# The last token group's projections traced whole before the early expert blocks, and the expert inputs loaded behind that group's weights

## The chip, the cores and the metric

The kernel runs on one core of one Trainium2 chip. The metric is the device time of one launch in microseconds, the median of three runs. A profiled execution is a further run of the same program under the hardware profiler.

## The reference, cut to what matters

One inference step of one layer of a hybrid decoder for 1024 prompt tokens and 32 sample tokens (8 sequences of 4), T = 1056 tokens of width 1024:

```
z = rmsnorm(x) @ w_in
h = x + [ rwkv7_mix(z_rwkv) | pool_mix(z_pool) ] @ w_out
xn = rmsnorm(h)
q = (xn @ peer_wq).reshape(tokens, 8 heads, 2, 128)
s1, s2 = q[:, :, 0] . keys[0],  q[:, :, 1] . keys[1]        # 128 keys each
v1, i1 = top_k(s1, 16);  v2, i2 = top_k(s2, 16)
sc, ci = top_k(v1 + v2 over all 256 pairs, 16)
expert = i1[ci // 16] * 128 + i2[ci % 16];  gate = softmax(sc)
act = gelu(u_tab[expert] . xn) * gate
h = h + sum over (8 heads x 16 experts) act * v_tab[expert]
h = h + (p @ ple_w) * sigmoid(rmsnorm(h) @ ple_gate_w)
y = rmsnorm(h)
```

So each token uses 128 of 16384 experts, and each expert is a row of u_tab and a row of v_tab, 1024 numbers each. Outputs are y for both sets of tokens and the new shift, wkv and pool states.

## The kernel before, in words

**Tiling and stages.** The 1056 tokens are the columns of most matmuls, in four groups (`GROUPS`, columns 0 to 288, 288 to 544, 544 to 800, 800 to 1056). The width of 1024 lies in 8 blocks of 128 partitions (`KB` = 8). A product that must be exact to fp32 is made as three matmuls of split operands: an operand is split into a part `hi` (a copy by ScalarE, ACT) and a rest `lo` or `elo` (a subtraction on VectorE, DVE, or on GpSimd, POOL), and the products hi·hi, hi·lo and lo·hi are summed (`mm3`, L649 to L660; `emm`, L1103 to L1110).

1. Stage a makes z for all tokens, stage b runs the wkv recurrence in chunks and leaves the mixed rows y in DRAM (`y_d`).
2. `phase_c(gi)` (from L680) takes one group of tokens: it loads y (L687), splits it, multiplies by the 8 column blocks of w_out (`wblock`, then `mm3`), adds the products into h (L700), normalises (L714), splits again and multiplies by the 16 column blocks of peer_wq; every 4 of these give two heads, whose scores against the keys (L743) go to DRAM (`sc_d`, L747). `wblock` loads pre-split weights from DRAM on the SyncE queue, SP (`whi`, L646, and `wlo`, L647). For the last six blocks of the last group (`b >= C3E`, `C3E` = 18) it loads unsplit weights (`eraw`, L1084) and splits them on the chip with `esplit`, the subtraction on POOL (`PTT`, L125).
3. `top` (from L749) takes one tile of up to 128 tokens: it reads the scores back (`scq`, L762), finds the 16 best of each head with DVE instructions (L765 to L770), the 16 best pairs, the gates, and, for the 672 "dense" tokens (columns below `GB`), the dense gate matrix. That matrix, 128 experts of a block by 128 blocks, is made for four tokens at a time, here called a quad: DVE builds one-hot factors (`ab`, L898) and two products (L899 and L900; the second, in two quads of three, on POOL, L125), PE multiplies them (8 matmuls, L903), ACT copies the result out (`gst`, L905), and every 32 tokens go to DRAM (`g_d`, L907). The tiles of dense tokens begin at columns 0, 128, 256, 288, 416, 544; the one at 544 has 128 tokens, 32 quads.
4. Expert blocks: there are 128 u-blocks of 128 experts and 16 groups of 8 v-blocks. A u-block (`ublock`, L1112 to L1116) splits 128 rows of u_tab (`eraw` from `uT`, 128x1024), makes 48 calls of the matmul line in `emm` against the normalised inputs `XH`, `XL` of the 672 dense tokens (two halves of 336 columns, shown as x2: 48 matmuls in all), and writes gelu of the sum to a tile `OT0` to `OT7` or `wt` (L1116). `ugate` (L1161) multiplies it by the dense gates, read back from DRAM (`gq`, L1164; L1167), and splits it (`wh` L1169 on ACT, `wl` L1171 on DVE). `vblock` (L1174) makes the 48 matmuls of a v-block from `wh` and `wl` of 8 u-blocks; the first v-block needs the gates of u-blocks 0 to 7.
5. The other 384 tokens fetch their expert rows one by one with indirect DMAs on POOL (L1219) and use DVE for the products (L1227 and L1236); this runs beside the expert blocks. A tail with the last gate and norms ends the kernel.

**What sets the order.** The kernel is written as Python generators. `merge` steps several of them in turn, each in proportion to its stated length, while the instructions are traced. The step loop (L1123 to L1150) does so for the stages: in step s the chunks of stage b, the tiles of `top` of group s − 2, and `phase_c(s - 1)`. A list scheduler then takes the traced instructions in traced order as priorities and places them per engine by a model of when their inputs are ready, so the order on an engine can differ from the traced one. Buffers come from pools with a fixed number of slots: `eraw` has 3, `ehi` and `elo` 2 each, the PSUM tiles `pd` of `emm` 2. The statement `with tc.issue_after(ins)` keeps the instructions traced inside it behind `ins` on the same queue.

**The place of the change.** In the last step (`step == NG`, 4) the tiles of group 2 are stepped to their end first; their pool is closed; then `phase_c(3)` (stated length 24) and `upre()`, which traces u-blocks 0 to 7, are merged (L1134 to L1141). Ahead of that, at the end of step 3, the 16 loads of `XH` and `XL` (128x672 each, 0.34 MB) are issued (L1147 to L1149). The loads come from `xh_d` and `xl_d`, where `phase_c(0)` to `phase_c(2)` have written the normalised, split inputs. After the step loop, `dense` traces u-blocks, gates and v-blocks.

Of the kernel before, what the change touches and what calls it, by code (L numbers as in the profile page):

```python
# [10 lines left out]
F32 = mybir.dt.float32  # L11
# [9 lines left out]
KB = D // 128  # L21
# [41 lines left out]
def body(ctx, tc, io):  # L63
    nc = tc.nc
# [12 lines left out]
    xh_d = dram.tile([128, KB, ND], F32, name="xh_d")  # L77
    xl_d = dram.tile([128, KB, ND], F32, name="xl_d")
    sc_d = dram.tile([sum(-(-(b - a) // 128) for a, b in GROUPS), 128, 16, 128], F32, name="sc_d")
    h2_d = dram.tile([128, KB, GT], F32, name="h2_d")  # L80
    wc_d = dram.tile([KB + 16, 128, 2, KB, 128], F32, name="wc_d")
# [380 lines left out]
    def bchunk(c, sp=None):  # L462
# [171 lines left out]
        PTT(yo, yo, fo, op=ALU.add)  # L634
        nc.sync.dma_start(y_d[:, :, pos:pos + tt], yo[:, :, :tt])

    def wblock(gi, b):
        if b >= C3E and gi == NG - 1:
            hi, lo = esplit(io["wq"][b - KB], PTT)
            return [(t[0], t[1]) for t in zip(*[(x[:, :HK], x[:, HK:]) for x in (hi, lo)])]  # L640
        out = []
        for i in range(1 if b < KB else 2):
            ks = slice(i * HK, (i + 1) * HK)
            hi = ws.tile([128, HK, 128], F32R, name="whi", bufs=3)
            lo = ws.tile([128, HK, 128], F32R, name="wlo", bufs=3)
            nc.sync.dma_start(hi.bitcast(F32), wc_d[b, :, 0, ks, :])  # L646
            nc.sync.dma_start(lo.bitcast(F32), wc_d[b, :, 1, ks, :])  # L647
            out.append((hi, lo))
        return out  # L649

    def mm3(ps, w, x, n):
# [257 lines left out]
    NG = len(GROUPS)  # L909
# [164 lines left out]
    NPRE = 8  # L1074
# [7 lines left out]
    def esplit(src, sub=TT):  # L1082
        raw = dr.tile([128, KB, 128], F32, name="eraw", bufs=3)
        nc.sync.dma_start(raw, src)  # L1084
        hi = dr.tile([128, KB, 128], F32R, name="ehi", bufs=2)
        ACT(hi, raw, AF.Copy)  # L1086
        lo = dr.tile([128, KB, 128], F32R, name="elo", bufs=2)
        sub(lo, raw, hi.bitcast(F32), op=ALU.subtract)  # L1088
        return hi, lo
# [28 lines left out]
    def upre():  # L1118
        for b in range(NPRE):
            ublock(b, PTT)  # L1120
            yield

    CL = [0, 24, 24, 24, 24]  # L1123
    for step in range(1, NG + 1):
        streams = []
        if step < NG:
            c_ = BC[step + 2:step + 4]
            streams.append((b_len(*c_), b_stream(*c_)))
        if 0 <= step - 2 < NG:
            streams.append((t_len(step - 2), t_stream(step - 2)))  # L1130
        if 0 <= step - 1 < NG:
            streams.append((CL[step], phase_c(step - 1)))
        if step == NG:
            for _ in streams[0][1]:  # L1134
                pass
            gstack.close()
            late = ctx.enter_context(tc.tile_pool(name="late", bufs=1, side="right", reuse_waits="tile"))
            gqp = ctx.enter_context(tc.tile_pool(name="gqp", bufs=2, side="right", reuse_waits="tile"))
            streams = [streams[1], (NPRE, upre())]
        merge(streams)  # L1140
        if step == NG - 1:  # L1141
            nc.sync.dma_start(io["wkv_p"], S[-1])
            pbx.close()
            dr = ctx.enter_context(tc.tile_pool(name="dr", bufs=1, side="right", reuse_waits="tile"))
            dps = ctx.enter_context(tc.tile_pool(name="dps", bufs=2, side="right", space=bass.MemoryType.PSUM, reuse_waits="tile"))
            XH, XL = xsplit()
            for k in range(KB):  # L1147
                nc.sync.dma_start(XH[:, k, :].bitcast(F32), xh_d[:, k, :])
                nc.sync.dma_start(XL[:, k, :].bitcast(F32), xl_d[:, k, :])  # L1149
            xs = [(XH[:, k, :], XL[:, k, :]) for k in range(KB)]  # L1150
    def gtop(col):
        for _ in top(tk, GB + col, min(128, GT - col)):
# [170 lines left out]
    XH, XL = xsplit()  # L1323
# [95 lines left out]
```

## Time and profile before

| | us |
|---|---|
| time before, median of 3 runs | 3339.67 |
| lowest and highest of them | 3336.93, 3353.06 |
| the profiled execution, device time | 3365.37 |
| its span in the trace | 3363.7 |
| mean granted TensorE clock in it | 0.968 |

| stage, us of the span | what runs |
|---|---|
| up to 1179 | stages a and b, `phase_c(0)` to `phase_c(2)`, the tiles of groups 0 and 1 up to the middle of tile 416 |
| 1179 to 1374 | rest of tile 416, `phase_c(3)`, tile 544, u-blocks 0 to 6 |
| 1374 to 1413 | last projections of `phase_c(3)`, u-blocks 7 and 8 |
| 1413 to 3205 | expert blocks, with the tiles of the 384 other tokens and then the gathers beside them |
| 3205 to 3364 | last expert blocks, tail |

How to read it: times are in microseconds from the start of the span unless marked ns. PE is TensorE, PEld its weight loads. A row of the timeline gives start, duration, engine, line, operation, output and input; what stands in brackets at its end is the time the engine was idle before it and what ended that wait. A row of the windows gives a stretch, its length, the busy time and number of instructions of each engine (PE, PEld, DVE, ACT, POOL, in this order), the granted TensorE clock, the busy share of the 16 DMA engines and GB/s.

### The profile page before, as it was taken

Reading aid. Unit: us, or ns where it says so; the run is one execution under the profiler, and the core shown is the slowest. Engines: PE = TensorE matmul, PEld = TensorE weight load, DVE = VectorE, ACT = ScalarE, POOL = GpSimd, SP = SyncE. Lnnn points to the kernel's source line nnn. Section 1 sums busy time; section 2 is a strip of 40 time slices with the busy share of each in tenths; the row PEclk is TensorE's granted clock in tenths of the full one; section 3 lists DMA queues with packets and bytes.
Section 4 is the critical chain, followed back from the end, with each engine's and each line's share of the span. In section 5 each row is a group of like instructions: output and inputs, shape, how many; then the busy total and the mean of one; then the engine's idle time right before and its main releaser. Section 6 shows DMA issues by size and latency. Waiting matters only on the chain.

```text
span 3363.7 us, 66962 instructions
## 1 busy us (share of the span) xinstructions
PE 3145.6 (94%) x26777; PEld 3006.4 (89%) x26777; DVE 2585.2 (77%) x5124; ACT 1128.8 (34%) x1734; POOL 1736.5 (52%) x1439
## 2 busy tenths in 40 slices
PE   8997799896998988899999999999999999999997
PEld 7886688786787877899999999999999999999997
DVE  6766322229799879899898888888889888888966
ACT  6452322223555555431221222222222222222243
POOL 5433232215446455327666665566566566666634
PEclk9998899997999989999999999999999999999998
DMA  4668544665776796739999999999999999999933
GB/s 160 203 219 195 145 130 127 204 191 149 235 217 201 232 317 204 244 109 371 343 330 332 343 349 328 333 334 339 337 336 349 326 330 342 338 329 337 323 107 127
DMA packets 448856, 879.89 MB, mean 262 GB/s; under 512 B 110240, under 2 KB 233376, under 8 KB 444064
## 3 DMA queue, kind: packets, MB, share of 16 engines
q1 hardware_dynamic: 337952, 472.91, 43.8%
q0 software_dynamic: 110592, 402.70, 32.9%
q8 instruction: 210, 3.44, 0.4%
q14 instruction: 102, 0.84, 0.1%
HBM read 754.89 MB, written 120.60 MB: 260 GB/s over the span
## 4 chain that ended last, share of the span: by engine, by line
PE 54%; DVE 7%; DMA 2%; issue 1%; ACT 0%; POOL 0%; SPq 0%; ACTq 0%; DVEq 0%; POOLq 0%
PE pd L1110 53%; DVE ab L898 1%; DMA row<-u,idx 1%; DVE elo L1088 1%; DVE oh L850 0%; DMA scq<-sc_d 0%; DMA eraw<-wq 0%; DVE OT L1316 0%; DVE ab L899 0%; DVE I L766 0%; DVE s L768 0%; DVE tg L1302 0%; DVE I L770 0%; DMA g_d<-gst 0%; DMA gq<-g_d 0%
## 5 line engine op out<-in xcount | busy, mean ns | idle before, releaser
L1219 POOL DMA_INDIRECT row<-v,idx x384 | 530.6, 1382 | 330.8 <-DVE po L1236 150.9
L1219 POOL DMA_INDIRECT row<-u,idx x384 | 542.5, 1413 | 274.9 <-DVE row L1227 107.4
L1086 ACT ACTIVATE ehi<-eraw 128x1024 fp32r<-128x1024 f32 x278 | 294.5, 1060 | 1095.9 <-PE pd L1110 976.8
L1110 PE MATMUL pd<-XH,elo 128*128 128x336 f32 x2176 | 515.3, 318 | 5.9 <-POOL elo L125 4.7
L1110 PE MATMUL pd<-XL,ehi 128*128 128x336 f32 x2176 | 515.1, 317 | 0.0
L1110 PE MATMUL pd<-XH,ehi 128*128 128x336 f32 x2176 | 512.4, 316 | 0.4 <-ACT ehi L1086 0.4
L1110 PE MATMUL pd<-wh,ehi 128*128 128x336 f32 (+1 forms) x2112 | 504.1, 317 | 6.6 <-DVE tg L1300 6.2
L1110 PE MATMUL pd<-wl,ehi 128*128 128x336 f32 (+1 forms) x2112 | 504.0, 317 | 0.0
L1110 PE MATMUL pd<-wh,elo 128*128 128x336 f32 (+1 forms) x2112 | 503.9, 317 | 0.2 <-DVE elo L1088 0.2
L1236 DVE SCALAR_TENSOR_TENSOR po<-row,act,po 128x1024 f32<-128x1024 f32 x381 | 488.5, 1282 | 6.8
L1227 DVE SCALAR_TENSOR_TENSOR row<-row,xt 128x1024 f32<-128x1024 f32 x384 | 455.7, 1219 | 9.7 <-DMA row<-u,idx 9.5
L1110 PEld LDWEIGHTS pd<-XH,elo 128*128 128x128 f32 x2176 | 373.5, 188 | 7.1 <-POOL elo L125 5.5
L1088 DVE TENSOR_TENSOR elo<-eraw,ehi 128x1024 fp32r<-128x1024 f32 x256 | 318.3, 1243 | 77.2 <-ACT ehi L1086 69.0
L1110 PEld LDWEIGHTS pd<-XH,ehi 128*128 128x128 f32 x2176 | 372.9, 189 | 0.9 <-ACT ehi L1086 0.6
L1110 PEld LDWEIGHTS pd<-XL,ehi 128*128 128x128 f32 x2176 | 371.3, 188 | 0.2
L1110 PEld LDWEIGHTS pd<-wh,ehi 128*128 128x128 f32 x2112 | 362.6, 188 | 7.6 <-issue 7.4
L1110 PEld LDWEIGHTS pd<-wh,elo 128*128 128x128 f32 x2112 | 362.7, 188 | 0.6 <-DVE elo L1088 0.5
L1110 PEld LDWEIGHTS pd<-wl,ehi 128*128 128x128 f32 x2112 | 362.8, 188 | 0.0
L125 POOL TENSOR_TENSOR ab<-ab,e 128x512 f16<-128x512 f16 x110 | 130.1, 1185 | 180.6 <-DVE ab L899 139.0
L657 PE MATMUL ps<-hi,whi 128*128 128x256 f32 (+1 forms) x592 | 185.7, 315 | 29.3 <-DMA whi<-wc_d 15.8
L1179 DVE TENSOR_TENSOR OT<-pd,OT 128x672 f32<-128x672 f32 x120 | 102.9, 857 | 140.7 <-PE pd L1110 139.8
L905 ACT ACTIVATE gst<-ps 128x512 f32<-128x512 f32 x168 | 174.9, 1089 | 85.5 <-PE ps L903 78.4
(428 smaller groups left out, 5526.9 us busy)
## 6 DMA issues: line engine op xcount, KB each, us to landing
eraw<-uT SPq DMA_DIRECT2D x128, 512.0 KB
eraw<-vP SPq DMA_DIRECT2D x128, 512.0 KB
g_d<-gst SPq DMA_DIRECT2D x21, 2048.0 KB
gq<-g_d SPq DMA_DIRECT2D x32, 1344.0 KB
whi<-wc_d SPq DMA_DIRECT2D x148, 256.0 KB
wlo<-wc_d SPq DMA_DIRECT2D x148, 256.0 KB
fdc<-fd SPq DMA_DIRECT2D x16, 896.0 KB
wc_d<-shi SPq DMA_DIRECT2D x40, 256.0 KB
```

Of the source, the lines that this page charges most:

```text
L125: nc.gpsimd.tensor_tensor(out, a, b, op=op)
L657: mm(ps[:, :n], whi[:, kk, :], xhi[:, k, :n], start=k == 0, stop=False)
L898: TT(ab[:, 0:4], iota16[:, None, :, :].to_broadcast([128, 4, EB, 2]), pairs(0, 4), op=ALU.is_equal)
L905: ACT(st[:, :, t2:t2 + 4].rearrange("p e t -> p t e"), v3(ps, 128), AF.Copy, scale=1.0 / GS)
L1086: ACT(hi, raw, AF.Copy)
L1088: sub(lo, raw, hi.bitcast(F32), op=ALU.subtract)
L1110: mm(ps[:, a, :n], w_[:, k, :], x_[:, s:s + n], start=first, stop=last)
L1179: TT(halves(OT[db]), ps[:, :, :NH], halves(OT[db]), op=ALU.add)
L1219: nc.gpsimd.indirect_dma_start(out=r[:m], out_offset=None, in_=io[tab], in_offset=bass.IndirectOffsetOnAxis(ap=idx[:m, hh, k:k + 1], axis=0))
L1227: STT(r[:m], r[:m], 1.0, xt[:m], op0=ALU.mult, op1=ALU.mult, accum_out=pre[:m, k:k + 1])
L1236: STT(po[:m], r[:m], act[:m, k:k + 1], po[:m], op0=ALU.mult, op1=ALU.add)
```

## The change: what it does

In the last step `phase_c(3)` is no longer merged with `upre()`: it is traced to its end, and then u-blocks 0 to 7 are traced. The 16 loads of `XH` and `XL` no longer stand in one row at the end of step 3; a new function `xload(k)` issues the pair of block k, and `wblock` calls it for each of the 8 w_out blocks of the last group, kept behind the weight load of that block on the SP queue. What is computed, and by which instructions, is the same; lines after the insertions have a number higher by 4 (`wblock`), 7 (up to the step loop) or 6 (after it).

```diff
--- before.py
+++ after.py
@@ -634,6 +634,10 @@
         PTT(yo, yo, fo, op=ALU.add)
         nc.sync.dma_start(y_d[:, :, pos:pos + tt], yo[:, :, :tt])
 
+    def xload(k):
+        nc.sync.dma_start(xs[k][0].bitcast(F32), xh_d[:, k, :])
+        nc.sync.dma_start(xs[k][1].bitcast(F32), xl_d[:, k, :])
+
     def wblock(gi, b):
         if b >= C3E and gi == NG - 1:
             hi, lo = esplit(io["wq"][b - KB], PTT)
@@ -644,8 +648,11 @@
             hi = ws.tile([128, HK, 128], F32R, name="whi", bufs=3)
             lo = ws.tile([128, HK, 128], F32R, name="wlo", bufs=3)
             nc.sync.dma_start(hi.bitcast(F32), wc_d[b, :, 0, ks, :])
-            nc.sync.dma_start(lo.bitcast(F32), wc_d[b, :, 1, ks, :])
+            l = nc.sync.dma_start(lo.bitcast(F32), wc_d[b, :, 1, ks, :])
             out.append((hi, lo))
+            if gi == NG - 1 and b < KB:
+                with tc.issue_after(l.ins):
+                    xload(b)
         return out
 
     def mm3(ps, w, x, n):
@@ -1136,7 +1143,9 @@
             gstack.close()
             late = ctx.enter_context(tc.tile_pool(name="late", bufs=1, side="right", reuse_waits="tile"))
             gqp = ctx.enter_context(tc.tile_pool(name="gqp", bufs=2, side="right", reuse_waits="tile"))
-            streams = [streams[1], (NPRE, upre())]
+            for _ in streams[1][1]:
+                pass
+            streams = [(NPRE, upre())]
         merge(streams)
         if step == NG - 1:
             nc.sync.dma_start(io["wkv_p"], S[-1])
@@ -1144,9 +1153,6 @@
             dr = ctx.enter_context(tc.tile_pool(name="dr", bufs=1, side="right", reuse_waits="tile"))
             dps = ctx.enter_context(tc.tile_pool(name="dps", bufs=2, side="right", space=bass.MemoryType.PSUM, reuse_waits="tile"))
             XH, XL = xsplit()
-            for k in range(KB):
-                nc.sync.dma_start(XH[:, k, :].bitcast(F32), xh_d[:, k, :])
-                nc.sync.dma_start(XL[:, k, :].bitcast(F32), xl_d[:, k, :])
             xs = [(XH[:, k, :], XL[:, k, :]) for k in range(KB)]
     def gtop(col):
         for _ in top(tk, GB + col, min(128, GT - col)):
```

PE, in the middle of tile 416 of `top`. `ab_14942` and `ab_14956` are the factors of two quads that follow each other, `pd_15845` is the sum of u-block 0 and `pd_15965` that of u-block 1. Before:

```order
L903 LDWEIGHTS ab_14942
L903 MATMUL ps_14941<-ab_14942 128x128
L1110 MATMUL pd_15845<-XH_15049,ehi_15848 128x336 x2
L1110 MATMUL pd_15845<-XL_15050,ehi_15848 128x336 x2
L1110 MATMUL pd_15845<-XH_15049,elo_15850 128x336 x2
...
L1110 MATMUL pd_15965<-XH_15049,ehi_15968 128x336 x2
L1110 MATMUL pd_15965<-XL_15050,ehi_15968 128x336 x2
L903 LDWEIGHTS ab_14956
L903 MATMUL ps_14955<-ab_14956 128x128
```

The same place now:

```order
L910 LDWEIGHTS ab_14942
L910 MATMUL ps_14941<-ab_14942 128x128
L910 LDWEIGHTS ab_14956
L910 MATMUL ps_14955<-ab_14956 128x128
```

All 48 matmuls of u-block 0 (24 rows of x2, the repeats left out) and the first four of u-block 1 stood between the two quads; now nothing does.

PE, at the last quad of tile 544, the last of all (`ab_15790` before, `ab_15774` now). `ps_16747` and `ps_16779` are two of the last wq projections of `phase_c(3)`, `ehi_16775` and `elo_16777` the split weights of one. Before:

```order
L903 LDWEIGHTS ab_15790
L903 MATMUL ps_15789<-ab_15790 128x128
L658 MATMUL ps_16779<-lo_16170,ehi_16775 128x256
L659 MATMUL ps_16779<-hi_16169,elo_16777 128x256
L657 MATMUL ps_16779<-hi_16169,ehi_16775 128x256
L657 MATMUL ps_16747<-hi_16169,whi_16743 128x256
```

Now, where `ps_16518` is one of the last wq projections, `ps_16640` the scores of the last, `pd_16656` the sum of u-block 0 and `pd_16713` that of u-block 1:

```order
L910 LDWEIGHTS ab_15774
L910 MATMUL ps_15773<-ab_15774 128x128
L750 MATMUL ps_16495<-keys_103,q_16362 128x128
L750 MATMUL ps_16503<-keys_103,q_16362 128x128 x4
L664 MATMUL ps_16518<-hi_15998,ehi_16514 128x256
L665 MATMUL ps_16518<-lo_15999,ehi_16514 128x256
L666 MATMUL ps_16518<-hi_15998,elo_16516 128x256
...
L1117 MATMUL pd_16656<-XH_15049,ehi_16659 128x336 x2
L1117 MATMUL pd_16656<-XL_15050,ehi_16659 128x336 x2
...
L1117 MATMUL pd_16713<-XH_15049,ehi_16716 128x336 x2
```

Before, 146 matmuls of projections, 16 of scores and 96 of u-blocks 7 and 8 stood between the last quad and the first v-block. Now it is 96 matmuls of projections, the scores, and the 432 of u-blocks 0 to 8. From the first v-block on, PE's order is the same in both, but for the transposes of the gathered tokens (L1246 before), which come 8 expert blocks earlier.

DVE, behind the last quad's factors. `OT0` to `OT3` are the outputs of u-blocks 0 to 3, `s2` and `V12` belong to the search for the best scores of the first tile of the gathered tokens. Before:

```order
L770 MAX_INDEX I12_18953<-V12_18952,s2_19002 128x8
L1167 TENSOR_TENSOR OT0_15900<-OT0_15900,gq_17386 128x672
L1167 TENSOR_TENSOR OT1_16020<-OT1_16020,gq_17386 128x672
L1167 TENSOR_TENSOR OT2_16140<-OT2_16140,gq_17386 128x672
L1167 TENSOR_TENSOR OT3_16351<-OT3_16351,gq_17386 128x672
```

Now:

```order
L1173 TENSOR_TENSOR OT0_16711<-OT0_16711,gq_17386 128x672
L776 MAX V12_18952<-s2_19022 128x8
L777 MAX_INDEX I12_18953<-V12_18952,s2_19022 128x8
...
L1177 TENSOR_TENSOR wl_17391<-OT0_16711,wh_17389 128x672
L772 MAX V12_18952<-scq_19032 128x8 x4
```

The gates of u-blocks 0 to 6 stood in one row; now they are spread among the searches. From the factors of the last quad to the rest `wl_17428` of u-block 7, which the first v-block needs, there were 83 DVE instructions before and are 254 now.

## The prediction

> **What bounds the kernel now.** I read the page first: its busy shares, then the chain of waits that ended last.
>
> ```profile
> PE 3145.6 (94%) x26777; PEld 3006.4 (89%) x26777; DVE 2585.2 (77%) x5124; ACT 1128.8 (34%) x1734; POOL 1736.5 (52%) x1439
> PE pd L1110 53%; DVE ab L898 1%; DMA row<-u,idx 1%; DVE elo L1088 1%; DVE oh L850 0%; DMA scq<-sc_d 0%; DMA eraw<-wq 0%; DVE OT L1316 0%; DVE ab L899 0%; DVE I L766 0%; DVE s L768 0%; DVE tg L1302 0%; DVE I L770 0%; DMA g_d<-gst 0%; DMA gq<-g_d 0%
> ```
>
> PE is busy 94% of the span, and 53% of the last chain is the expert matmuls of L1110. An average over stages can mislead, so the next view is the windows, cut at the stages around the change.
>
> ```profile
> 1179.00:1239.40 60.40, 46.23 (x359) 41.74 (x360) 40.02 (x83) 29.98 (x36) 29.80 (x22) 0.80 0.99 333
> 1239.40:1373.60 134.20, 113.13 (x900) 105.50 (x899) 128.71 (x545) 69.57 (x100) 72.66 (x75) 0.92 0.70 218
> 1373.60:1413.00 39.40, 36.70 (x277) 36.02 (x277) 26.74 (x109) 19.32 (x28) 11.93 (x5) 1.00 0.91 317
> 1413.00:1550.00 137.00, 135.36 (x876) 134.56 (x875) 124.69 (x522) 45.63 (x62) 52.01 (x56) 1.00 0.51 180
> 1550.00:3205.00 1655.00, 1655.00 (x10783) 1654.96 (x10782) 1445.22 (x1719) 400.16 (x475) 1042.67 (x747) 1.00 0.92 335
> ```
>
> Between 1239.4 and 1373.6 us, while DVE searches scores and builds the quads of tile 544, DVE is busy 128.71 of 134.20 us and PE 113.13: DVE paces. From 1373.6 on PE paces: 36.70 of 39.40, then 135.36 of 137.00, then all of 1655. So the kernel ends a fixed time after PE reaches its first v-block; what comes before counts only by when that is.
>
> The same windows with the expert tile `pd` alone (columns PE, PEld, DVE, ACT) show what PE does beside DVE's work:
>
> ```profile
> 1239.40:1373.60 134.20, 45.56 (x255) 40.76 (x254) 0.00 (x0) 4.38 (x6) 0.92 0.70 218
> 1373.60:1413.00 39.40, 16.13 (x99) 15.29 (x100) 0.00 (x0) 0.73 (x1) 1.00 0.91 317
> 1550.00:3205.00 1655.00, 1653.11 (x10759) 1652.36 (x10758) 97.73 (x114) 79.22 (x111) 1.00 0.92 335
> ```
>
> In the DVE-paced stretch 45.56 us of PE's work is 255 expert matmuls, 5.3 u-blocks of 48: work PE would need later anyway, done for nothing under DVE. The last row prices an expert matmul where PE is full: 1653.11/10759 = 0.154 us, so a block of 48 costs 7.38 us.
>
> Two timeline views show the other side: u-block 0 starts ahead of quads that DVE waits for. PE, POOL, then DVE:
>
> ```profile
> 1214.86 0.91 PE L1110 MATMUL pd<-XH,ehi 128*128 128x336 f32 x2
> 1221.01 0.93 PE L1110 MATMUL pd<-XH,elo 128*128 128x336 f32 x2 [4.68 <-POOL elo L125]
> 1230.41 1.09 PE L903 MATMUL ps<-ab 128*128 128x128 f16 x16
> 1412.61 0.47 PE L1110 MATMUL pd<-wh,ehi 128*128 128x336 f32 x2
> ```
>
> ```profile
> 1218.61 4.68 POOL L125 TENSOR_TENSOR elo<-eraw,ehi 128x1024 fp32r<-128x1024 f32 x2
> 1233.22 4.10 POOL L125 TENSOR_TENSOR lo<-y,hi 128x256 fp32r<-128x256 f32 x4
> ```
>
> ```profile
> 1231.15 3.81 DVE L898 TENSOR_TENSOR ab<-iota,e 128x1024 f16<-128x1024 f16 x2 [13.70 <-PE ps L903]
> ```
>
> PE holds the next quads until 1230.41; DVE, with all three `ab` slots in use, idles 13.70 us. The v-blocks (`pd<-wh`) begin at 1412.61.
>
> **The change part by part.** The profiled execution took 3365.37 us, 25.7 more than the median of the runs, 3339.67. I make the sum against the profiled one and carry the difference over unchanged.
>
> *Term A, from the last quad to the first v-block.* The chain of waits there, before:
>
> ```profile
> 1373.13 0.43 PE ps L903 x7
> 1374.75 7.94 DMA g_d<-gst
> 1385.78 11.28 DMA eraw<-wq
> 1401.10 0.12 PE ps L657
> ```
>
> The last quad ends at 1373.13 + 0.43 = 1373.56, so the stretch lasts 1412.61 − 1373.56 = 39.05 us. By the order it holds 146 projection matmuls at 0.12 (17.5), 16 score matmuls, put at the same 0.12 (1.9), and two u-blocks (14.8): 34.2, so 4.9 us are waits, where the 11.28 us load of a wq block ended late. After the change it holds 96 projection matmuls (11.5), about 20 score matmuls (2.4) and nine u-blocks (9 × 7.38 = 66.4): 80.3. Waits: the wq loads now stand far ahead, but nine loads of uT follow one another through three `eraw` slots. Bounds: 0, and 12, one load of 11.28 exposed whole; I take 5, as before. So 85.3, which is **+46** (from 80.3 − 39 = +41 to 92.3 − 39 = +53).
>
> *Term B, when the last quad comes.* The u-blocks gone from the DVE-paced part can bring it earlier in three ways.
>
> The 13.70 us stall goes. What is late next: two subtractions of wq blocks now stand on POOL among the products of tile 416's quads. One costs 4.68/2 = 2.34 us, the two 4.7; DVE has other quads in hand, so I charge 3. And y's split (4.10 us on POOL) with the first block's projection behind it, 36 matmuls at 0.12 (4.3), ran partly under that stall; behind the last quad of tile 416, DVE waits for it: 8.4 together, of which I charge 7. That leaves 13.7 − 3 − 7, about 4 (bounds 13.7, and 13.7 − 4.7 − 8.4 = 0.6, nearly nothing).
>
> Then the six POOL subtractions that leave the stretch. Some DVE instructions there take far longer than their median:
>
> ```profile
> L125 POOL TENSOR_TENSOR elo<-eraw,ehi 128x1024 fp32r<-128x1024 f32 x6 | 14.6, 2426 | 5.6 <-ACT ehi L1086 5.5
> ```
>
> ```profile
> L898 DVE TENSOR_TENSOR ab<-iota,e 128x1024 f16<-128x1024 f16 x32 | 27.6, 869 | 0.1
> L850 DVE TENSOR_TENSOR oh<-cF,CF 128x256 f32<-128x256 f32 x16 | 12.0, 757 | 0.3
> L900 DVE TENSOR_TENSOR ab<-ab,e 128x512 f16<-128x512 f16 x11 | 6.9, 624 | 0.0
> ```
>
> ```profile
> L898 DVE TENSOR_TENSOR ab<-iota,e x32: 664/678/2437, 1286.6 to 1368.4; 128x1024 f16<-128x1024 f16 x32
> L850 DVE TENSOR_TENSOR oh<-cF,CF x16: 412/492/2147, 1263.5 to 1371.0; 128x256 f32<-128x256 f32 x16
> L900 DVE TENSOR_TENSOR ab<-ab,e x11: 406/416/2148, 1292.3 to 1369.3; 128x512 f16<-128x512 f16 x11
> ```
>
> Above the medians (678, 492 and 416 ns) the three groups lost 27.6 − 32 × 0.678 = 5.9, 12.0 − 16 × 0.492 = 4.1 and 6.9 − 11 × 0.416 = 2.3: together 12.3 us, and the longest L898 took 2437 ns, as long as one subtraction (mean 2426). POOL runs other instructions there as well, so not all of the excess leaves with them. I take 8; bounds 0 and 14.6, all six subtractions.
>
> [...]
>
> Last, DVE's idle time in the stretch, 134.20 − 128.71 = 5.5 us: I count none of it, at most all.
>
> Term B is then −4 − 8 = **−12**, from 0 to −(13.7 + 14.6 + 5.5) = −34. Slower than before it can't be by more than a little: the order has nearly the same DVE instructions between the two tiles' last quads (399 against 396), and the waits it adds are those charged.
>
> *Term C, behind the first v-block.* PE's order is the same there. The gathers may start some eight blocks earlier, since their first DVE products stand earlier; they are worth little, because PE is full beside them and before the tail waits only this once:
>
> ```profile
> 3325.46 0.66 PE L1110 MATMUL pd<-wh,ehi 128*128 128x384 f32 x1 [5.70 <-DVE tg L1300]
> 1513.90 1.22 DVE L1227 SCALAR_TENSOR_TENSOR row<-row,xt 128x1024 f32<-128x1024 f32 x1 [3.40 <-DMA row<-u,idx]
> ```
>
> Zero. The respread `XH` and `XL` loads: SP issues the same transfers, and their first reader, u-block 0, moves from 1214.86 to behind the last quad, so nobody waits for them: zero. Should they hold up the weights beside them on the queue, the projections wait under DVE's work.
>
> *Cover.* The gates of u-blocks 0 to 7 must be ready for the first v-block. DVE passed 412 instructions between the last quad and the first gather product:
>
> ```profile
> 1373.60:1513.90 140.30, 118.69 (x582) 1.00 0.50 169
> DVE OT L1167 <- DMA gq<-g_d: 9.0, 2, 8.2
> ```
>
> That is 118.69/412 = 0.288 us an instruction. `wl` of u-block 7 is now the 254th behind the last quad: 73 us if nothing waits. But u-block 0 ends some 25 us after the last quad (projections and one block), and 196 DVE instructions stand from its gate on: 25 + 196 × 0.288 = about 82 us, against PE's 85. The cover is thin, 3 us; the 9.0 us wait for `gq` falls inside the 25.
>
> Sum: +46 − 12 + 0 = **+34 us**: 3365 becomes 3399 profiled, and the median 3340 becomes 3373. The unknowns' ends give 41 − 34 = +7 and 53 − 0 = +53.
>
> **The rivals.** A difference under 0.5%, 16.7 us, is about what a measurement of this kernel can tell from no change.
>
> 1. *Not slower: all of the DVE-paced time is won.* If stall, subtractions and idle time go whole, the last quad comes 34 us earlier and the loss is 39 to 41: +5, about 3345. It decides once the last quad comes 29 us or more earlier. For it: the lengths 2437 and 2426 match, and 13.70 is one wait. Against: y's split still has to run, and POOL's products of the quads stay. Chance 0.18.
> 2. *Faster.* For −17 us the last quad would have to come 63 us earlier, or the expert blocks would have to lose waits that I don't see. DVE's own 128.71 us less 12 leaves 116 of 134, which speaks against; what speaks for it is only the idle POOL and the 25.7 us between the profiled run and the median, whose place I can't see. Chance 0.08.
> 3. *Deeper loss: DVE comes late with the gates.* With a cover of 3 us, a DVE that meets both the 9.0 us wait for `gq` and POOL's subtractions of nine blocks (each 2.43, beside it) holds the first v-block by 12 to 20 us: +46 to +54, 3386 to 3394. It decides as soon as `wl` of u-block 7 comes more than 85 us behind the last quad. PE's clock could add to it: it was granted 0.80 where PE was busy 46.23 of 60.40. [...] Chance 0.17.
>
> That the change does nothing is excluded: the order shows nine u-blocks behind the last quad.
>
> **How the numbers follow.** The forecast, +34 with its own range 3357 to 3386, has 0.57. Rival 3 ends slower by over 0.5% too: 0.57 + 0.17 = 0.74. Rival 1 is within 0.5%: 0.18. Rival 2: 0.08. The range leaves out rival 2 and reaches to rival 1 and the upper bound: 3344 to 3393.
>
> **What would show it.** Right: no long DVE wait before tile 416's last quads; the last quad at about 1361; nine u-blocks in one run of some 66 us, ending at the first v-block near 1446; the DVE-paced stretch with fewer long L898. Wrong: a last quad before 1345 (term B), PE waiting over 12 us inside the run of u-blocks (term A's waits, or rival 3, by whether `elo` or `wl` ended them), or a v-block stretch of another length than before (term C).

## The result

Six runs of the changed kernel have a median of 3389.73 us (3386.29 to 3391.15), six of the kernel before 3344.05 (3336.93 to 3353.06). The ratio is 1.0129, 95% interval 1.0112 to 1.0146: slower by 43 us by the ratio; the two medians lie 45.7 us apart. Forecast were +34 and 3373, with 3344 to 3393 as the range. The measured time is inside it, near its upper end, and above the 3357 to 3386 that the forecast gave as its own.

The profiled execution of the changed kernel has a span of 3385.7 us. Its page, busy shares and the lines of the chain that ended last:

```profile
PE 3154.9 (93%) x26777; PEld 3013.1 (89%) x26777; DVE 2589.9 (76%) x5124; ACT 1127.6 (33%) x1731; POOL 1741.4 (51%) x1439
PE pd L1117 55%; DMA whi<-wc_d 1%; DVE ab L905 1%; PE ps L910 1%; PE ps L664 1%; DVE ab L906 1%; PE ps L486 1%; PE ps L666 1%; DVE oh L857 1%; PE ps L665 1%; PE ps L750 0%; DVE gl L860 0%; DMA scq<-sc_d 0%; DVE I L773 0%; DVE OT L1322 0%
```

No engine's share has moved by more than one per cent of the span, and L1117 is the former L1110. The page alone would not show where 43 us went. The timeline does, by three marks on PE: the last quad, the first u-block, the first v-block.

```profile
1345.71 0.67 PE L910 MATMUL ps<-ab 128*128 128x128 f16 x7
1360.74 0.56 PE L1117 MATMUL pd<-XH,ehi 128*128 128x336 f32 x2
1433.59 0.47 PE L1117 MATMUL pd<-wh,ehi 128*128 128x336 f32 x2
```

The last quad ends at 1346.38 and the first v-block starts at 1433.59: 87.2 us against 39.05. The windows of the DVE-paced part and of the part behind the last quad, then the second of them for the tile `pd` alone:

```profile
1211.20:1346.40 135.20, 91.80 (x679) 81.32 (x679) 127.42 (x554) 57.09 (x87) 62.03 (x70) 0.77 0.69 220
1346.40:1433.60 87.20, 82.44 (x555) 80.66 (x555) 68.25 (x343) 32.36 (x44) 34.72 (x27) 1.00 0.50 172
1550.00:3205.00 1655.00, 1655.00 (x10788) 1654.96 (x10787) 1420.62 (x1696) 401.39 (x481) 1032.73 (x734) 1.00 0.91 331
```

```profile
1346.40:1433.60 87.20, 68.14 (x433) 66.53 (x434) 0.00 (x0) 5.74 (x8) 1.00 0.50 172
```

Of the 87.2 us behind the last quad, 68.14 are expert matmuls, at full clock, with PE busy 82.44; before it was 16.13 of 39.40. The 45.56 us of expert matmuls that ran beside DVE's work are no longer there, and the DVE-paced part is no shorter for it: 135.2 us against 134.2.

For a comparison of profiles, a second one of the kernel before was taken (run `e1_before_again` below). Marks on DVE: the last state update of the recurrence, which both kernels reach by the same instructions, and the first addition into h of the last group. Before, in the second profile:

```profile
1151.61 0.42 DVE L611 TENSOR_TENSOR S<-ps,S 128x256 f32<-128x256 f32 x1 [3.35 <-PE ps L486]
1219.17 3.82 DVE L898 TENSOR_TENSOR ab<-iota,e 128x1024 f16<-128x1024 f16 x2 [13.26 <-PE ps L903]
1227.45 0.75 DVE L700 TENSOR_TENSOR h<-ps,h 128x256 f32<-128x256 f32 x2
```

```profile
1360.43 0.57 PE L903 MATMUL ps<-ab 128*128 128x128 f16 x7
1399.50 0.47 PE L1110 MATMUL pd<-wh,ehi 128*128 128x336 f32 x2
```

After:

```profile
1144.41 0.42 DVE L611 TENSOR_TENSOR S<-ps,S 128x256 f32<-128x256 f32 x1 [1.54 <-PE ps L486]
1211.22 0.76 DVE L707 TENSOR_TENSOR h<-ps,h 128x256 f32<-128x256 f32 x2 [5.46 <-PE ps L666]
```

From these marks and the spans, in us, with the experiments of the next section beside them:

| kernel | update to first h | to end of last quad | to first v-block | update to first v-block | from there to the end |
|---|---|---|---|---|---|
| before, first profile | 77.0 | 134.2 | 39.0 | 250.2 | 1951.1 |
| before, second (e1) | 75.9 | 133.5 | 38.5 | 247.9 | 1948.5 |
| after | 66.8 | 135.2 | 87.2 | 289.2 | 1952.1 |
| e2, u-blocks behind alone | 69.2 | 146.3 | 66.6 | 282.1 | 1955.3 |
| e3, loads spread alone | 67.6 | 142.0 | 46.9 | 256.5 | 1951.3 |
| e5, four u-blocks behind | 67.7 | 128.5 | 69.7 | 265.9 | 1953.9 |
| e6, u-blocks behind tile 416 | 70.6 | 144.1 | 37.9 | 252.6 | 1952.2 |
| e7, subtractions on DVE | 74.4 | 151.9 | 23.7 | 250.0 | 1954.8 |
| e8, changed, POOL busier | 68.8 | 149.0 | 82.9 | 300.7 | 1950.0 |
| e9, changed, loads later | 68.2 | 132.8 | 83.0 | 284.0 | 1952.5 |
| e10, e6 and searches held | 69.5 | 145.6 | 36.8 | 251.9 | 1948.4 |
| e11, e7 and searches held | 74.5 | 148.6 | 22.5 | 245.6 | 1957.4 |
| e13, before, first search held | 75.7 | 111.0 | 47.7 | 234.4 | 1961.9 |

The fourth column carries the result: +41.3 us between the second profile of before and the changed kernel. The last column is 1948 to 1955 in all but two. One of e6's twelve runs took 14664.7 us; its ratio leaves that run out, and its median, 3352.4, would be 3352.21 without it.

### The profile page after: what moved, and what is told of

It reads as the page before. It is cut to its first block, busy times and chain, and to the rows that moved or that the text cites. A ratio compares the mean times of both kernels' runs of the same rounds, so it can differ in the third digit from the quotient of the medians.

```text
span 3385.7 us, 66965 instructions
## 1 busy us (share of the span) xinstructions
PE 3154.9 (93%) x26777; PEld 3013.1 (89%) x26777; DVE 2589.9 (76%) x5124; ACT 1127.6 (33%) x1731; POOL 1741.4 (51%) x1439
## 4 chain that ended last, share of the span: by engine, by line
PE 59%; DVE 9%; DMA 2%; ACT 1%; issue 1%; POOL 0%; DVEq 0%; ACTq 0%; SPq 0%; POOLq 0%
PE pd L1117 55%; DMA whi<-wc_d 1%; DVE ab L905 1%; PE ps L910 1%; PE ps L664 1%; DVE ab L906 1%; PE ps L486 1%; PE ps L666 1%; DVE oh L857 1%; PE ps L665 1%; PE ps L750 0%; DVE gl L860 0%; DMA scq<-sc_d 0%; DVE I L773 0%; DVE OT L1322 0%
## 5 line engine op out<-in xcount | busy, mean ns | idle before, releaser
L1117 PE MATMUL pd<-XH,elo 128*128 128x336 f32 x2176 | 512.0, 317 | 3.4 <-POOL elo L125 2.5
L1117 PE MATMUL pd<-XL,ehi 128*128 128x336 f32 x2176 | 512.8, 316 | 0.0
L1117 PE MATMUL pd<-XH,ehi 128*128 128x336 f32 x2176 | 510.2, 315 | 0.4 <-ACT ehi L1093 0.2
L1117 PE MATMUL pd<-wh,ehi 128*128 128x336 f32 (+1 forms) x2112 | 503.9, 317 | 6.4 <-DVE tg L1306 6.4
L1117 PE MATMUL pd<-wh,elo 128*128 128x336 f32 (+1 forms) x2112 | 503.9, 317 | 3.7 <-DVE elo L1095 3.4
L1117 PE MATMUL pd<-wl,ehi 128*128 128x336 f32 (+1 forms) x2112 | 503.5, 317 | 0.0
L1117 PEld LDWEIGHTS pd<-XH,elo 128*128 128x128 f32 x2176 | 372.1, 188 | 4.5 <-POOL elo L125 3.1
L1117 PEld LDWEIGHTS pd<-XH,ehi 128*128 128x128 f32 x2176 | 371.3, 188 | 1.2 <-ACT ehi L1093 0.5
L1117 PEld LDWEIGHTS pd<-XL,ehi 128*128 128x128 f32 x2176 | 370.1, 188 | 0.2
L1117 PEld LDWEIGHTS pd<-wh,ehi 128*128 128x128 f32 x2112 | 362.1, 188 | 7.2 <-issue 7.0
L1117 PEld LDWEIGHTS pd<-wh,elo 128*128 128x128 f32 x2112 | 362.1, 188 | 5.0 <-DVE elo L1095 4.2
L1117 PEld LDWEIGHTS pd<-wl,ehi 128*128 128x128 f32 x2112 | 362.3, 188 | 0.1
```

What stands on the lines that cost most here:

```text
L1117: mm(ps[:, a, :n], w_[:, k, :], x_[:, s:s + n], start=first, stop=last)
```

## The experiments

Ratios are to the kernel before, which ran beside each; its median was 3350.86 to 3351.69 us there.

**The kernel before again.** No edit; one more profiled execution.

> The kernel before, unchanged, for a second profile. Both theories below start from the two profiles' common part: up to about 1160 us both kernels issue the same DVE instructions, and the first profile of before was 18 us later there (1162.4 against 1144.4). If that was chance, this profile has the state update of 1162.4 near 1145, the device time is 3337 to 3350, and the 13.70 us wait of DVE before tile 416's quads is there again. If it belongs to the program, the device time is again about 3365.

Measured: 3349.68 us, the update at 1151.61, the wait of 13.26 us there again. So most of the first profile's lateness at that mark, 10.8 of 18 us, was chance, and the stall belongs to the program. That the changed kernel is another 7 us earlier there (1144.41) can't be told from the scatter: the other kernels stand between 1144 and 1157.

**The first half of the change alone.**

```diff
-            streams = [streams[1], (NPRE, upre())]
+            for _ in streams[1][1]:
+                pass
+            streams = [(NPRE, upre())]
```

> Only the first half of the change: u-blocks traced behind phase_c(3), the XH and XL loads in one row as before. By the order 407 expert matmuls and no projection stand between the last quad and the first v-block (before: 96 and 146). Theory of the lost cover (each expert matmul behind the last quad costs 0.154 us, each projection matmul 0.12, and the DVE-paced part wins about 10 us because the stall before tile 416's quads is gone): 407 x 0.154 = 62.7 + 5 of waits = 68 against 39, +29 - 10 = +19 us, ratio about 1.006. Rival, the loads (the pairs of XH and XL between the weights make the last group's projections late): nothing of the loss is here, ratio 0.997 to 1.001.

Measured: 3384.85, ratio 1.0099 (1.0085 to 1.0114). The loss is mostly here, against the rival. The stretch behind the last quad came as worked out (66.6, expected 68); the last quad came 6 us later than before instead of 10 earlier, so the loss is 33 and not 19.

**The second half alone.** The changed kernel, with the wq blocks merged with the u-blocks.

```diff
-            for _ in streams[1][1]:
-                pass
-            streams = [(NPRE, upre())]
+            for _ in range(KB):
+                next(streams[1][1])
+            streams = [(CL[step] - KB, streams[1][1]), (NPRE, upre())]
```

> Only the second half of the change: the XH and XL loads spread behind the last group's w_out weights; phase_c(3) runs its 8 w_out blocks first, and its 16 wq blocks are then merged with the u-blocks as before. By the order 144 expert matmuls and 166 of projections stand behind the last quad. Theory of the lost cover: 22 + 20 + 2 + 5 = 49 against 39, +10, and as u-block 0 again stands among tile 416's quads (behind quad 123 of 168) the stall is not won: ratio 1.000 to 1.004. Rival, the loads: the whole loss is here, ratio about 1.012.

Measured: 3358.95, ratio 1.0026 (1.0016 to 1.0035), as the theory of the lost cover had it. One part was wrong: u-block 0 stands among tile 416's quads again, and yet there was no stall (67.6 us to the first h). In this trace its matmuls stand there in pieces of at most 8 between quads; before, 52 in a row.

**Half the u-blocks behind.** The same, with four of the eight merged.

```diff
+            U_ = upre()
+            half = (next(U_) for _ in range(4))
+            merge([(CL[step] - KB, streams[1][1]), (4, half)])
+            streams = [(NPRE - 4, U_)]
```

> The changed kernel with the first four u-blocks merged into the 16 wq blocks and four traced behind them. By the order 288 expert matmuls and 145 of projections stand behind the last quad. Theory of the lost cover: 44.3 + 17.4 + 2 + 5 = 69 against 39, +30, less up to 10 for the stall: ratio 1.006 to 1.009, half way between the second-half kernel and the changed kernel. Rival, the loads: they are spread as in the changed kernel, ratio about 1.012.

Measured: 3370.23, ratio 1.0049 (1.0032 to 1.0066), between e3 and the changed kernel, under the expected 1.006 to 1.009. With 3, 6 and 9 u-blocks behind the last quad (e3, e5, the changed kernel) 46.9, 69.7 and 87.2 us lie there; worked out were 49, 69 and 85.

**The u-blocks kept behind tile 416's quads.** The kernel before with:

```diff
-        emm(ps, esplit(io["uT"][b], sub), xs, DP)
+        w = esplit(io["uT"][b], sub)
+        with tc.issue_after(QL[416]) if b < NPRE else nullcontext():
+            emm(ps, w, xs, DP)
```

where `QL[416]` is the tile's last matmul of L903.

> The kernel before with one rule more: the matmuls of u-blocks 0 to 7 are kept behind the last quad of tile 416; the merge and the loads are as before. By the order no u-block stands among tile 416's quads, six start under tile 544's, and 106 projection matmuls, 16 of scores and 96 expert matmuls stand behind the last quad. Theory of cover and stall: the stall goes (DVE's 76 us from the last state update to the first addition into h of the last group become 67, as in the changed kernel) and 12.7 + 1.9 + 14.8 + 5 = 34 follows the last quad against 39: -9 - 5 = -14 us, ratio about 0.996. Rival, the stall is worth nothing (PE only catches up later what it did early, and DVE waits for that instead): ratio 0.999 to 1.001.

Measured: 3352.4, ratio 1.0000 (0.9992 to 1.0009). The theory failed: 5 us fewer to the first h, 11 more from there to the last quad. The rival's number came, but the stall was only shortened: DVE still waits 13.1 us in all for tile 416's quads up to the first h, against 20.8 before and 4.4 in the changed kernel.

**Those subtractions on DVE.** The kernel before with `ublock(b)` for `ublock(b, PTT)` in `upre`.

> The kernel before with the subtractions of u-blocks 0 to 7 on DVE instead of POOL. Six of them lie in the DVE-paced part: +6 x 1.24 = 7.4 us of DVE work. By the order only 48 projection matmuls, 8 of scores and 50 expert matmuls stand behind the last quad: 5.8 + 1 + 7.7 + 5 = 20 against 39, -19. Theory that POOL's subtractions hold DVE for their whole length: 14.6 come back, so the last quad moves by 7.4 - 14.6 = -7 and the sum is -26, ratio 0.992. Rival, they hold DVE for little of it (3 us, as the groups of L898, L850 and L900 show between the first two kernels): last quad +4, sum -15, ratio 0.9955.

Measured: 3352.86, ratio 1.0006 (0.9997 to 1.0016): both missed. Behind the last quad only 23.7 us are left, as expected, but the last quad comes 17 us later. From the update to the last quad DVE is busy 191.3 us here against 177.8 before, so 13.5 of these 17 are more work on DVE.

**More work on POOL.** The changed kernel with, in `phase_c`:

```diff
         for j in range(HEADS // 2):
+            if gi == NG - 1 and j:
+                for i in range(8):
+                    dm = work.tile([128, maxn], F32, name="sq", bufs=1)
+                    PTT(dm[:, :256], h[:, i, :256], q[:, i % 4, :256], op=ALU.subtract)
```

> The changed kernel with 24 more subtractions of 128x256 on POOL among tile 544's quads, whose results nobody reads (about 0.83 us each, 20 us). By the order 48 projection matmuls instead of 96 stand behind the last quad: 5.8 + 1 + 66.4 + 5 = 78 against 87, -9. Theory that POOL's work holds DVE for its whole length: the last quad comes up to 20 us later, sum +11, ratio about 1.016 to the kernel before, and the mean L905, L857 and L907 grow by 20 us in all. Rival, it holds DVE for a quarter of it at most: last quad +5, sum -4, ratio about 1.0115.

Measured: 3401.07, ratio 1.0143 (1.0128 to 1.0158), between the two. The groups of DVE in the DVE-paced part, second profile of before, after, and this kernel; then the added subtractions (21 of the 24 are in the trace):

```profile
L898 DVE TENSOR_TENSOR ab<-iota,e 128x1024 f16<-128x1024 f16 x32 | 27.0, 849 | 0.1
L899 DVE TENSOR_TENSOR ab<-ab,e 128x512 f16<-128x512 f16 x33 | 18.1, 560 | 0.0
L850 DVE TENSOR_TENSOR oh<-cF,CF 128x256 f32<-128x256 f32 x16 | 12.0, 758 | 0.3
L900 DVE TENSOR_TENSOR ab<-ab,e 128x512 f16<-128x512 f16 x11 | 6.9, 624 | 0.0
```

```profile
L905 DVE TENSOR_TENSOR ab<-iota,e 128x1024 f16<-128x1024 f16 x32 | 26.9, 845 | 2.6 <-PE ps L910 2.5
L906 DVE TENSOR_TENSOR ab<-ab,e 128x512 f16<-128x512 f16 x32 | 17.4, 548 | 0.0
L857 DVE TENSOR_TENSOR oh<-cF,CF 128x256 f32<-128x256 f32 x16 | 9.7, 619 | 0.4 <-ACT cF L834 0.2
L907 DVE TENSOR_TENSOR ab<-ab,e 128x512 f16<-128x512 f16 x11 | 7.1, 643 | 0.0
```

```profile
L909 DVE TENSOR_TENSOR ab<-iota,e 128x1024 f16<-128x1024 f16 x32 | 27.9, 879 | 2.8 <-POOL sq L125 2.3 <-PE ps L914 0.5
L910 DVE TENSOR_TENSOR ab<-ab,e 128x512 f16<-128x512 f16 x32 | 25.8, 811 | 0.0
L861 DVE TENSOR_TENSOR oh<-cF,CF 128x256 f32<-128x256 f32 x16 | 10.1, 644 | 0.3 <-ACT cF L838 0.2
L911 DVE TENSOR_TENSOR ab<-ab,e 128x512 f16<-128x512 f16 x11 | 6.7, 613 | 0.0
L125 POOL TENSOR_TENSOR sq<-h,q 128x256 f32<-128x256 f32 x21 | 21.0, 999 | 9.5 <-ACT q L749 9.3
```

The four groups sum to 64.0 us before, 61.1 after and 70.5 here, 9.4 more than after. Not all of this is the added work's: four of the subtractions of wq (10.1 us on POOL) stand in the stretch here, two (4.9 us) after. Row by row the trace says more. A product of these groups that starts while POOL runs an instruction ends shortly behind the end of that instruction: in the median 0.28 us behind it for L910, L911 and L861, 0.55 for L909. A product that starts beside none takes 0.41 us, and 0.68 for L909. In the DVE-paced part of the changed kernel, 31 of the 35 products that start so end at the same two distances; the other four end inside one POOL product of 2.67 us. So most of them last as long as what is left of the POOL instruction, and the total depends on how many start inside one: the 19 products that started inside an added subtraction took 5.6 us more than the shortest of their groups, 27% of the 21.0 us. The last quad also comes later because more searches stand ahead of it (427 DVE instructions of the order against 399), so the time of the whole kernel does not measure this.

**The pairs of XH and XL later.** The changed kernel with:

```diff
-            if gi == NG - 1 and b < KB:
-                with tc.issue_after(l.ins):
-                    xload(b)
+        if gi == NG - 1 and KB <= b < 2 * KB:
+            with tc.issue_after(l.ins):
+                xload(b - KB)
```

> The changed kernel with the pairs of XH and XL behind the weights of wq blocks 0 to 7 instead of w_out blocks 0 to 7. PE's order at the last quad is the same as in the changed kernel. Theory that the pairs hold up the weights beside them and so the projections that DVE waits for (6.9 us for the additions into h): the time from the first of these additions to the last quad falls from 135 to 125 to 130, ratio about 1.010 to the kernel before. Rival, their place does not matter: ratio 1.012 to 1.014, the 135 stay.

Measured: 3385.45, ratio 1.0104 (1.0089 to 1.0118): the expected 1.010, but not by the expected way. The DVE-paced part is 132.8 us long, not 125 to 130, and DVE's wait for the projections is still 6.4 us against 6.9. Of the 5 us to the first v-block, 4 lie behind the last quad (83.0 against 87.2), where PE waits 0.5 us in all against 4.7. That the place of the loads does this is likely; how is not shown.

**Stall and searches both held.** e6 with the later searches of the gathered tokens kept behind the last product on DVE:

```diff
-    for col in range(128, GT, 128):
-        gtop(col)
+    with tc.issue_after(QD[544]):
+        for col in range(128, GT, 128):
+            gtop(col)
```

> The kernel with the u-blocks' matmuls kept behind tile 416's last quad, and the score searches of the second and third tile of gathered tokens kept behind the last quad's product on DVE. Theory that the DVE instructions ahead of the last quad set when it comes: without this rule the order had 421 DVE instructions from the first addition into h of the last group to the last quad and they took 144 us; before it was 396 and 133.5, 0.42 us each. Now there are 401: 136 us, and as 34 us follow the last quad and the stall is gone, the ratio is 0.997 to 0.998. Rival, the stall is worth nothing: ratio 0.9995 to 1.001 as without the rule.

Measured: 3351.87, ratio 0.9997 (0.9988 to 1.0006): the rival. DVE instructions ahead of the last quad are not what made e6 longer. What DVE waited for in the DVE-paced part, before (second profile), after, and in this kernel (line, what it waits for, us in total, times, longest):

```profile
DVE h L700 <- PE ps L659: 0.8, 1, 0.8
```

```profile
DVE h L707 <- PE ps L666: 6.9, 2, 5.5
DVE ab L905 <- PE ps L910: 2.5, 2, 1.5
```

```profile
DVE h L702 <- PE ps L659: 5.2, 2, 3.2
DVE ab L900 <- PE ps L905: 1.6, 2, 1.0
```

Where the one long wait is gone or shorter, DVE waits for the first w_out projections, 5 to 7 us against 0.8: it seems that they were finished unseen under it.

**The same rule on e7.** The edit is that of e10.

> The kernel with the u-blocks' subtractions on DVE, and the same searches kept behind the last quad. 406 DVE instructions instead of 419 stand ahead of the last quad, five of them the subtractions. Theory of the DVE instructions: 13 x 0.42 = 5.5 us less than without the rule, where the first v-block came 2 us later than before: ratio 0.998 to 0.999. Rival, the first v-block comes when PE has done its work, whatever DVE does first: ratio 1.000 to 1.001 as without the rule.

Measured: 3355.27, ratio 1.0018 (1.0007 to 1.0029), both missed. The first v-block came 2 us earlier than before, and the rest took 1957.4 us.

**The first search held.** The kernel before with `gtop(0)` inside `with tc.issue_after(QD[544])`.

> The kernel before with the search of the first tile of gathered tokens kept behind the last quad's product on DVE: 222 DVE instructions instead of 396 stand between the first addition into h of the last group and the last quad, 170 instead of 83 from there to the gates of u-block 7, and 603 instead of 413 to the first gather. Theory of cover: with DVE's work gone from there, PE's own work (111 us busy of 133) paces, the last quad comes 20 to 30 us earlier, 180 projection and 96 expert matmuls follow it (43 us with waits), DVE needs 170 x 0.288 = 49, so the first v-block comes 10 to 20 us earlier: ratio 0.994 to 0.997. Rival, the gates then come late, or the gathers end late: ratio 1.000 or more, with PE waiting for wl or elo, or for the gathered rows at the end.

Measured: 3345.69, ratio 0.9981 (0.9972 to 0.9991), faster than both kernels by a little, and short of the expected 0.994 to 0.997. Its DVE-paced part and the first v-block:

```profile
1223.70:1334.70 111.00, 103.38 (x864) 96.45 (x862) 100.35 (x283) 66.95 (x92) 63.07 (x59) 0.97 0.77 239
```

```profile
1382.37 0.47 PE L1111 MATMUL pd<-wh,ehi 128*128 128x336 f32 x2
```

The theory of cover holds up to there: 111 us instead of 133.5, PE busy 103.38 of it, and 234.4 us from the update to the first v-block, 13.5 fewer. Of these, 6 are left in the median. The gathers end later, by the last row that DVE writes for them, in the second profile of before and here:

```profile
3190.24 1.28 DVE L1248 TENSOR_TENSOR row<-pt,row 128x512 f32<-128x512 f32 x2
```

```profile
3217.02 1.28 DVE L1250 TENSOR_TENSOR row<-pt,row 128x512 f32<-128x512 f32 x2
```

That the later gathers took it is argued from these two rows, not shown by a run of its own.

## Why the prediction was right, step by step

**What bounds the kernel: right.** Every kernel ends 1948 to 1955 us after its first v-block, but for e11 and e13 (1957.4 and 1961.9). In both, searches were moved behind the last quad on DVE; e10 moves the same ones as e11 and has 1948.4, so that alone does not explain them. The forecast stood on this fixed distance.

**The base: right to carry over, for a reason not known then.** The first profiled execution of before was late in a part that both kernels share; the second has a span of 3348.0. The plain difference of the two first spans, 22 us, would have told half the loss. For the same reason the signs given as times of the span came early: the last quad at 1346.38 instead of 1361, the first v-block at 1433.59 instead of 1446, and the update 18 us earlier than in the first profile.

**Term A, +46: +48.7** (87.2 − 38.5). The same sum (0.154 for an expert matmul, 0.12 for one of a projection or of scores, 5 of waits) was made for eight other kernels (e2, e3, e5 to e8, e10, e13) and came within 5 us in each. Its part for the scores was misread: 13 score matmuls follow the last quad and not 20, and each is two rows of 0.11 us in the trace; this makes 2.8 us where I had 2.4. PE's waits in the run of u-blocks were these, of the assumed 5:

```profile
PE pd L1117 <- POOL elo L125: 2.5, 2, 1.3
PE pd L1117 <- DVE elo L1095: 0.9, 1, 0.9
```

**Term B, −12: −7.4** (202.0 us from the update to the last quad against 209.4). The sum was near by luck, for its make-up was wrong in both parts. The windows from the update to the first h, before (second profile) and after:

```profile
1151.60:1227.50 75.90, 59.84 (x526) 55.27 (x522) 49.64 (x104) 37.94 (x48) 33.27 (x26) 0.84 0.92 309
1144.40:1211.20 66.80, 50.77 (x467) 44.97 (x461) 51.63 (x103) 38.63 (x48) 32.06 (x26) 0.80 0.93 300
```

With the DVE-paced part behind them, DVE is busy 49.64 + 128.14 = 177.8 us before and 51.63 + 127.42 = 179.1 after. Its idle time falls from 31.6 to 23.0 us. So all of the gain is waits, and none is DVE work that became shorter.

- The stall: gone, as forecast, and the first h is 9.1 us earlier. I charged y's split and the first projection with 7; DVE's waits for projections and quads behind the first h, 9.4 us against 0.8, are that charge and a little more. But u-block 0 was not the whole of the stall. What DVE waited for tile 416's quads up to the first h, before, after, in e2 and in e10:

```profile
DVE ab L898 <- PE ps L903: 20.8, 8, 13.3
```

```profile
DVE ab L905 <- PE ps L910: 4.4, 5, 2.3
```

```profile
DVE ab L898 <- PE ps L903: 12.5, 7, 5.3
```

```profile
DVE ab L900 <- PE ps L905: 13.8, 8, 6.1
```

  In e2 and e10 no u-block stands among these quads, and DVE still waits 12.5 and 13.8 us for them; in both the 16 loads of `XH` and `XL` stand in one row, and the changed kernel has them spread. The same line runs through all profiles: from the update to the last quad DVE idles 22 to 24 us in the five kernels whose loads are spread or later, and 29 to 37 in the others. A likely way is the SP queue, where the row stands ahead of y's load (issued 55 us after the update with the row, 45 to 50 without) and of a transfer of `g_d` that frees a slot of `gst`: ACT waits for that one 5.4 us before (second profile; 5.3 in the first) and 5.2 in e2, and not at all in the changed kernel. No run tests this way by itself. As e6 and e10 keep most of these waits, they do not show what the stall alone is worth.
- POOL's subtractions: I took 8 for six. Two, those of wq, still stand in the stretch (4.9 us of 14.6 on POOL), the four groups gave 2.9, and DVE's busy time as a whole gave nothing. The long L905 are still there too, 26.9 us against 27.0 in the group. That the longest L898 took as long as one subtraction was chance: it starts 0.47 us into one of 2.35 us and ends 0.55 us behind it. Nor is there a fixed gain for each: e6 has eight of them in the stretch (19.5 us on POOL), and its groups sum to 61.1 as in the changed kernel; e2 has six (15.2 us), and 69.0.
- What u-blocks among the quads cost DVE's path stays open. The last quad comes 215.1 us after the update in e10, with seven of them ahead of it, but 215.6 in e2, with half of one, and 196.3 in e5, with three. So the gain of the changed kernel can't be put down to their removal; the loads and the order of projections and searches differ as well.

**Term C, 0: +3.6** by these profiles (1952.1 against 1948.5), +1.0 by the first; inside the scatter of the table. Most of the 3.6 can be seen: behind the first v-block PE waits longer for DVE's splits of weights, the longest time 10.8 us after it. Before (second profile) and after:

```profile
PE pd L1110 <- DVE elo L1088: 0.6, 2, 0.4
```

```profile
PE pd L1117 <- DVE elo L1095: 3.4, 2, 2.3
```

The gathers did start earlier and end 18 us earlier (3171.90 against 3190.24), and it was worth nothing, as forecast.

**The loads off the path: wrong.** I had them at zero because nobody waits for their data soon. That asked only who reads them, not what stands behind them on the queue; in the kernels with the row DVE idles at least 4.8 us longer ahead of the last quad, as told under term B. What e3 loses to the first v-block, 8.6 us, is not theirs: 8.4 of it lie behind the last quad (46.9 against 38.5), where more matmuls stand. Later in the queue (e9) the median is 4 us below the changed kernel's and the ratio 0.0025 lower, with intervals that overlap.

**The rivals.** Not slower, and faster: out by the interval. (The first took term A at 39 to 41, where the sum has 46.) The deeper loss by late gates is the one whose numbers fit, 3386 to 3394 against 3389.73, and its sign came: `wl` of u-block 7 ends at 1437.74, 91.4 us behind the last quad, later than the 85 named, after DVE lost 15.3 us waiting for scores. These are that `wl` on DVE and its first reader on PE:

```profile
1436.90 0.84 DVE L1177 TENSOR_TENSOR wl<-OT,wh 128x672 fp32r<-128x672 f32 x1
1440.61 0.47 PE L1117 MATMUL pd<-wl,ehi 128*128 128x336 f32 x2
```

Yet the first v-block was not held: it reads this rest only in its last eighth, 94.2 us behind the last quad, and no wait for `wl` is in PE's list. So the cover held by 2.9 us, for a reason that the working had missed: it asked for all of the gates at the start of the v-block. Of that rival's mechanism only the waits for `elo` under term C came.

The clock was lower, 0.77 in the DVE-paced part against 0.94, and 1.00 behind the last quad. That it cost nothing is not shown, since DVE waited 9.4 us for PE in that part against 0.8; but e10, at a clock of 0.93, waited 6.8 there, so little of it can be the clock's.

The 9 us by which 34 fell short of 43 are the sum of these: 2.7 in A, 4.6 in B, 3.6 in C, less what the profiles differ from the medians.

## What to carry to other kernels

Where one engine paces a stretch and another paces all that follows, count what each order leaves for the second engine behind the first one's last hand-over: that sum alone (432 expert matmuls instead of 96) told the sign and most of the size here. A long wait that such an order removes is not yet a gain: look for what was done unseen under it, because here it was what the engine waited for next (5 to 7 us for the first w_out projections against 0.8), and for what else would have held it at the same place. Of a transfer that nobody reads soon, ask also what stands behind it on its queue. Compare two profiles from a mark that both programs reach by the same instructions, and not by their spans.

## What the runs showed of the hardware

- The granted clock was lower in the DVE-paced part where PE was busy for less of it: 0.94 with 111.11 of 133.50 us busy in the second profile of before, 0.77 with 91.80 of 135.20 in the changed kernel, 0.97 with 103.38 of 111.00 in e13. The part in the second profile of before, all tiles and then `pd` alone:

```profile
1227.50:1361.00 133.50, 111.11 (x898) 103.57 (x897) 128.14 (x545) 69.55 (x99) 73.35 (x75) 0.94 0.70 219
```

```profile
1227.50:1361.00 133.50, 45.26 (x255) 40.43 (x253) 0.00 (x0) 4.40 (x6) 0.94 0.70 219
```

  After, without them, the 679 matmuls that stand there take 91.80 us busy; the 643 other ones of before took 65.85.
- Of the products on DVE in the groups L898, L899, L850 and L900 that started while POOL ran an instruction, most ended shortly behind its end: 30 of 33 in the first profile of before and 31 of 35 in the changed kernel, 0.55 us behind it for L898 (there L905) and 0.28 for the other three. The longest L898 in the first profile starts 0.47 us into a POOL subtraction and ends 0.55 us behind it; those that start beside no POOL instruction take 0.68 (median):

```profile
1286.61 2.44 DVE L898 TENSOR_TENSOR ab<-iota,e 128x1024 f16<-128x1024 f16 x1
1286.14 2.35 POOL L125 TENSOR_TENSOR elo<-eraw,ehi 128x1024 fp32r<-128x1024 f32 x1
```

  Summed over a stretch, what POOL's work costs DVE is no fixed share of it: 5.6 us for the 21.0 added in e8, and the same four groups sum to 61.1 us with 19.5 us of weight subtractions on POOL (e6) and to 69.0 with 15.2 (e2).
- The profiled execution of one program was 15.7 us longer than another of the same (3363.7 and 3348.0); 10.8 of these lie before the last state update, far from the change.
